# Weight products of one decoder layer: three products of 256 columns instead of one of 512 and one of 256

## Chip, core and metric

The kernel runs on one core of a Trainium2 chip. The metric is the device time of one execution in microseconds. Beside it stands the profile of one execution, taken by the hardware profiler, with the times of all instructions. PE is TensorE (matmuls), PEld its weight loads, DVE is VectorE, ACT is ScalarE, POOL is GpSimd.

## What is computed

One layer of a decoder on 256 tokens with 4096 channels, float32. The input is RMS-normalised and multiplied by `w_in` (4096 x 21024); the columns of the product are split into the inputs of two token mixers, of their gates and of the merge:

```
proj = einsum('btd,dn->btn', rms_norm(x, pre_norm_g), w_in)
o_a  = sliding_window_attention(q_a, k_a, v_a, sinks)         # 32 heads of 64
y_a  = einsum(o_a * silu(z_a), w_pa)                          # 2048 -> 4096
o_b  = rms_norm(gated_delta_rule(q_b, k_b, v_b, beta, g))     # 16 heads of 128
y_b  = einsum(o_b * silu(z_b), w_pb)                          # 2048 -> 4096
merged = sigmoid(gate_a) * y_a + sigmoid(gate_b) * y_b
out  = x + rms_norm(einsum(merged, w_o), post_norm_g)         # 4096 -> 4096
```

The q, k and v of branch B pass a causal convolution over four tokens and a SiLU first. Time goes almost wholly into the products with the four weight matrices, 492 MB read from HBM.

## The kernel before

**Precision by halves.** TensorE multiplies in the type `F32R`, which keeps fewer bits than float32. So every operand is split into a high part, rounded to `F32R`, and a low part, the rest. A product of weight w and activation h is then hi(w)hi(h) + hi(w)lo(h) + lo(w)hi(h). The activations of 256 tokens lie as one tile of 512 columns for each k tile: columns 0 to 255 the high part (`m[:, 0:T]`), columns 256 to 511 the low part (`m[:, T:512]`). Their names are `hT` for the input, `gbs` and `gas` for the gated outputs of the branches.

**The weight product.** `gemm` (L199) computes 512 output columns, 4 column tiles of 128, for all 256 tokens. The 128 x 128 tile of the weights is the stationary operand, the activations move. The contraction runs over 32 k tiles for `w_in` and 16 for `w_pa` and `w_pb`. `load` fetches four k tiles in one DMA of 1 MB, on SP's queue; `split` (L162 on) makes the two parts of two k tiles at a time: ACT casts the high part (L170), DVE subtracts for the low part (L171). Two k tiles times four column tiles are a unit, after which `tick` lets the side work advance by a stage. For each weight tile there are two matmuls, called a pair here:

- high part of the weights, all 512 columns of the activations, into all 512 columns of a PSUM bank (L227): columns 0 to 255 gather hi x hi, columns 256 to 511 gather hi x lo;
- low part of the weights, the 256 high columns, into columns 256 to 511 of the same bank (L228).

In the last k tile the two change places (L224, L225). One product occupies four banks, one for each column tile; the pool `psmain` has five, `psside` three for the side work.

**Folding.** The two halves of a bank have to be added. `fold` (L233) copies the right half to SBUF on ACT (L236), and either adds it to the left half on DVE (L238), or copies the left half too (L240) and adds the two in SBUF (L241). `scale_tokens` (L245) then multiplies four column tiles at once by `R`, the reciprocal root of each token's mean square, which is computed beside the first product (R is written at L319). The callers are the convolutions (`conv_silu`), the gates (`gate_silu`, `gate`), the inputs of the attention (`kv_chain`, `qa_chain`), and the merge of the branches (L703 to L708 and `merge`).

**Order of the work.** The Python order of the calls with priorities sets the order on each engine. `urgent(2)` puts the splitting of weights ahead of everything else, `urgent(1)` the folding ahead of the side work. The side work (chains such as `keys_chain`, `values_chain`, `heads_chain`) runs in stages between the units. The products come in this order: 16 of branch B's inputs with its mixer beside them (the substitution of the delta rule, L501 and L502, is DVE work beside the units 6 to 14 of a product), 8 of `gate_b`, 8 of `w_pb`, one for k and v of branch A and 8 for its gates and queries with the attention beside them, then `gate_a` in turn with `w_pa`. That makes 41 column blocks of `w_in` and 16 of the two branch projections. The output projection `w_o` has code of its own (L856 to L858): there the activations are stationary and 512 columns of the weights move.

Of the kernel before, what the change touches and what calls it, by code (L numbers as in the profile page):

```python
# [25 lines left out]
NEG = -1e30  # L26
WARM = (5, 2)  # products that warm the tensor engine up before and behind the first of x
PACED = 4  # the first pieces of x (and blocks of weights) that are queued in a fixed order
STEP = 1.5  # vector work of the substitution let in beside a unit of the weight product
STEP_UNITS = (6, 14)  # units of a product beside which the substitution runs  # L30
HELD = 8  # k tiles of the last output columns kept back, so that the first token tile ends early

# [21 lines left out]
def tile_hybrid_mixer(  # L54
# [20 lines left out]
    wp = ctx.enter_context(tc.tile_pool(name="weights", bufs=3, side="left"))  # L75
    ev = ctx.enter_context(tc.tile_pool(name="evac", bufs=4, side="left"))
    mp = ctx.enter_context(tc.tile_pool(name="psmain", bufs=5, space=PSUM))
    sp = ctx.enter_context(tc.tile_pool(name="psside", bufs=3, space=PSUM))
    dp = ctx.enter_context(tc.tile_pool(name="scratch", bufs=1, space=bass.MemoryType.DRAM))
# [7 lines left out]

# [1 line left out]
    ident = cp.tile([P, P], F32, name="ident")  # L89
# [37 lines left out]

# [1 line left out]
    chains = []  # L129
# [30 lines left out]

# [1 line left out]
    def split(raw, extra=False):  # L162
# [36 lines left out]
    def gemm(w, col0, mov, nkt, first=False):  # L199
        ps = [mp.tile([P, 512], F32, name="mm") for _ in range(4)]  # L200
        for k4 in range(nkt // 4):
            raw = load(w, k4, slice(col0, col0 + 512), (4, 2)[k4] if first and k4 < 2 else 1)
            if first:
                x_load(k4 + 1)
            if first and k4 == 0:
                parts = [split_first(raw[:, 2 * u:2 * u + 2], 2 * u) for u in range(2)]
            for u in range(2):
                if first and k4 == 0:
                    hi, lo = parts[u]
                elif first and k4 < PACED:  # L210
                    i = 4 * k4 + 2 * u - 3
                    with tc.issue_after(x_ins[i][0]), tc.issue_after(x_ins[i][1]):
                        hi, lo = split(raw[:, 2 * u:2 * u + 2])
                else:
                    hi, lo = split(raw[:, 2 * u:2 * u + 2])
                order = [(nt, kk) for nt in range(4) for kk in range(2)]
                if first and k4 == 0:
                    order = [(nt, kk) for kk in range(2) for nt in range(4)]
                for nt, kk in order:
                    c = slice(nt * P, nt * P + P)  # L220
                    kt = 4 * k4 + 2 * u + kk
                    m = mov(kt)
                    if kt == nkt - 1:
                        PE.matmul(ps[nt][:, T:512], lo[:, kk, c], m[:, 0:T], start=False, stop=False, skip_group_check=True)  # L224
                        PE.matmul(ps[nt], hi[:, kk, c], m, start=False, stop=True, skip_group_check=True)  # L225
                    else:
                        PE.matmul(ps[nt], hi[:, kk, c], m, start=(kt == 0), stop=False, skip_group_check=True)  # L227
                        newest["product"] = PE.matmul(ps[nt][:, T:512], lo[:, kk, c], m[:, 0:T], start=False, stop=False, skip_group_check=True).ins  # L228
                unit[0] = 2 * k4 + u
                tick()  # L230
        return ps

    def fold(dst, ps):  # L233
        with urgent(1):
            cr = ev.tile([P, T], F32, name="cr")
            S.copy(cr, ps[:, T:512])  # L236
            if dst is None:
                V.tensor_tensor(cr, ps[:, 0:T], cr, op=ALU.add)  # L238
            else:
                S.copy(dst, ps[:, 0:T])  # L240
                V.tensor_tensor(dst, dst, cr, op=ALU.add)  # L241
        return cr

    def scale_tokens(ap):
        V.tensor_tensor(ap, ap, mid(R, ap.shape[1]), op=ALU.mult)  # L245

# [9 lines left out]

# [1 line left out]
    gbf = gb.rearrange("p a b -> p (a b)")  # L258
# [64 lines left out]
    def start_chain():  # L323
# [53 lines left out]
        S.activation(beta, ab[:, :, 0:16], AF.Sigmoid)  # L377
        # softplus(z) = max(z, 0) + 2 atanh(e / (2 + e)), e = exp(-|z|)
        z = ws.tile([P, 2, H_B], F32, name="z")
# [21 lines left out]
        yield 11  # L401
        # exp of the running sums (second chunk) and of the sums behind (first chunk)
        pt = sp.tile([P, 512], F32, name="sd")
# [5 lines left out]

# [1 line left out]
    cin = ws.tile([P, 4, 260], F32, name="cin")  # L411
# [4 lines left out]
    def conv_silu(ps, tbase, dst):  # L416
        for nt in range(4):
            fold(cin[:, nt, 4:260], ps[nt])
        scale_tokens(cin[:, :, 4:260])
        for nt in range(4):  # L420
# [11 lines left out]
    def gate_silu(ps, dst, pool):  # L432
        for nt in range(4):
            fold(dst[:, nt], ps[nt])
        scale_tokens(dst)
        sg = pool.tile([P, 4, T], F32, name="sg")
        S.activation(sg, dst, AF.Sigmoid)
        V.tensor_tensor(dst, dst, sg, op=ALU.mult)

    def keys_chain(st, ps):  # L440
# [4 lines left out]
        yield 4 if h0 else 8  # L445
        # decays exp(sum of g over (s, c]), zero for c < s
        dec = ws.tile([P, 2, 4, P], F32, name="dec")
# [33 lines left out]
        G.tensor_tensor(nk.rearrange("p a b -> p (a b)"), k2.rearrange("p a b -> p (a b)"), phalf, op=ALU.pow)  # L481
        # inverse of I + B: 32 x 32 diagonal blocks by substitution, one system in a partition
        d1 = dp.tile([4, 8, 32, 32], F32, name="d1", bufs=2)
# [35 lines left out]
        yield 3  # L519
        # the rest by the nilpotent series over blocks  # L520
        X = ws.tile([P, 2, 4, P], F32, name="blx")
# [80 lines left out]
    def queries_chain(st, ps):  # L602
# [26 lines left out]
        for ch in range(2):  # L629
# [15 lines left out]
            yield 1  # L645
        # rms norm of o = o' / sqrt(128 (q2 + eps)), the factor taken under the root
        V.tensor_scalar(q2, q2, P * EPS, P * EPS * EPS, op0=ALU.mult, op1=ALU.add)
# [34 lines left out]

# [1 line left out]
    def gate(ps, dst):  # L684
        for nt in range(4):
            fold(dst[:, nt], ps[nt])
        scale_tokens(dst)
        S.activation(dst, dst, AF.Sigmoid)
# [14 lines left out]
    for c in range(8):  # L703
        ps = gemm(w_pb, 512 * c, lambda kt: gbs[:, kt], KTB)
        for nt in range(4):
            y = fold(None, ps[nt])
            with urgent(1):
                V.tensor_tensor(m[c][:, nt], m[c][:, nt], y, op=ALU.mult)  # L708
    gspool.__exit__(None, None, None)
    gbpool.__exit__(None, None, None)  # L710

# [1 line left out]
    gapool = tc.tile_pool(name="gapool", bufs=1, side="right")  # L713
# [8 lines left out]
    def kv_chain(ps):  # L722
        for nt in range(4):
            fold(kv[:, nt], ps[nt])
        scale_tokens(kv)
        nc.sync.dma_start(kx[0:64], kv[64:128, 0:2])
        nc.sync.dma_start(kx[64:128], kv[0:64, 0:2])
        yield 3
        pt = side((2, T))
        for c in range(2):  # L730
            for t in range(2):
                PE.transpose(pt[:, c, t * P:t * P + P], kv[:, 2 + t, c * P:c * P + P], ident)
        S.copy(vt, pt)
# [7 lines left out]
    def qa_chain(st, ps):  # L741
        q = ap.tile([P, 4, T], F32, name="q")
        for nt in range(4):
            fold(q[:, nt], ps[nt])
        scale_tokens(q)
        yield 2
# [5 lines left out]
    def heads_chain(st, nt):  # L752
        g, q, gz = st["g"], st["q"], st["gz"]
        hs = slice(8 * g + 2 * nt, 8 * g + 2 * nt + 2)
        s = ap.tile([P, 2, 384], F32, name="s", bufs=2)
        # the two heads of a pair hold different rows of the array and alternate
        pts = [sp.tile([P, 512], F32, name="sd") for _ in range(2)]
# [48 lines left out]

# [1 line left out]
    ps = gemm(w_in, OFF_GA, movh, KT)  # L808
# [11 lines left out]
    def merge(c):  # L820
        ps = gemm(w_pa, 512 * c, lambda kt: gas[:, kt], KTB)
        for nt in range(4):
            y = fold(None, ps[nt])
            with urgent(1):
                V.tensor_tensor(y, y, sa[c][:, nt], op=ALU.mult)
                V.tensor_tensor(m[c][:, nt], m[c][:, nt], y, op=ALU.add)

# [15 lines left out]

# [1 line left out]
    op_ = ctx.enter_context(tc.tile_pool(name="outp", bufs=1, side="left"))  # L845
# [105 lines left out]
```

## Time and profile before

| what | value |
|---|---|
| time, median of 3 runs | 2700.98 us (2700.91 to 2701.2) |
| span of the profiled execution, first to last instruction | 2699.4 us |
| PE busy | 2685.1 us, 15294 matmuls |
| PEld busy | 2331.5 us, 15294 weight loads |
| DVE busy | 1640.3 us |
| ACT busy | 1277.8 us |
| mean granted TensorE clock | 0.999 |
| mean HBM traffic | 184 GB/s |

The profiled execution's own time is its span, 1.6 us below the median of the runs. A row of a group of instructions gives line, engine, operation, output<-inputs, shapes and count, then busy time and the mean duration of one in ns, then the engine's idle time just before them and what ended it. The records of successive matmuls overlap (a mean of 393 ns for one of 512 columns, with the next one starting some 230 ns behind it); how fast they follow each other is read from their start times. A few per cent of the matmul records are missing.

### The profile page before, as it was taken

To read this page: it belongs to the slowest core of one execution; us is meant where nothing else is said; L and a number is where in the kernel's file an instruction comes from. 1 tells how busy PE (TensorE), PEld (TensorE's weight loads), DVE (VectorE), ACT (ScalarE), POOL (GpSimd) and SP (SyncE) were. 2 spreads that over 40 slices of the span, in tenths; PEclk is the share of its full clock that TensorE was granted. 3 is DMA by queue.
4 is the path that set the end of the run, shared out by engine and by line. 5 is a ranking of instruction groups with operands and counts; after the bars stand their busy time and mean duration, and the time that the engine had idled before them with its cause. 6 is when DMAs were issued, how large, how long until landed. Compare 5 with 4: busy or idle time off the path is not lost.

```text
span 2699.4 us, 37887 instructions
## 1 busy us (share of the span) xinstructions
PE 2685.1 (99%) x15294; PEld 2331.5 (86%) x15294; DVE 1640.3 (61%) x2273; ACT 1277.8 (47%) x1866; POOL 38.5 (1%) x58
## 2 busy tenths in 40 slices
PE   9999999999999999999999999999999999999998
PEld 8888888888888888888888888888888888888886
DVE  7785876776776454555555665666555555644445
ACT  6445545545545444444444554555444445443433
POOL 0100100000000000000000000000000000000000
PEclk9999999999999999999999999999999999999999
DMA  8554554655555655566565455455555555765555
GB/s 269 168 180 157 181 176 157 195 162 171 182 175 165 194 188 187 188 190 191 193 194 188 156 178 167 156 186 169 191 187 187 189 192 186 248 230 188 187 187 172
DMA packets 261856, 499.90 MB, mean 185 GB/s; under 512 B 21936, under 2 KB 23088, under 8 KB 261040
## 3 DMA queue, kind: packets, MB, share of 16 engines
q1 hardware_dynamic: 260528, 495.37, 57.3%
q8 instruction: 120, 1.97, 0.3%
q10 hardware_dynamic: 1152, 2.10, 0.2%
q14 instruction: 56, 0.46, 0.0%
HBM read 491.93 MB, written 5.24 MB: 184 GB/s over the span
## 4 chain that ended last, share of the span: by engine, by line
PE 93%; DVE 6%; issue 1%; ACT 0%; DMA 0%; POOL 0%; SPq 0%; DVEq 0%; POOLq 0%; ACTq 0%
PE mm L227 47%; PE mm L228 25%; PE mm L857 4%; PE mm L858 4%; PE mm L856 4%; DVE lo L171 2%; PE mm L225 2%; DVE pr L501 1%; PE mm L224 1%; DVE xs L502 1%; PE sd L762 1%; PE sd L797 1%; PE sd L546 0%; PE sd L787 0%; DVE c L427 0%
## 5 line engine op out<-in xcount | busy, mean ns | idle before, releaser
L227 PE MATMUL mm<-hT,hi 128*128 128x512 f32 x5084 | 1790.2, 393 | 0.1
L171 DVE TENSOR_TENSOR lo<-raw,hi 128x1024 fp32r<-128x1024 f32 x909 | 1111.3, 1224 | 901.5 <-ACT hi L170 900.3
L170 ACT CAST hi<-raw 128x1024 fp32r<-128x1024 f32 x909 | 952.6, 1049 | 1281.0 <-PE mm L227 1049.6
L228 PE MATMUL mm<-hT,lo 128*128 128x256 f32 x5084 | 1436.1, 283 | 1.2 <-DVE lo L171 0.6
L227 PEld LDWEIGHTS mm<-hT,hi 128*128 128x128 f32 x5084 | 954.4, 188 | 198.9 <-issue 7.9
L228 PEld LDWEIGHTS mm<-hT,lo 128*128 128x128 f32 x5084 | 960.5, 189 | 14.9 <-DVE lo L171 7.0
L858 PE MATMUL mm<-hi,ms 128*128 128x512 f32 x508 | 200.9, 396 | 0.0
L857 PE MATMUL mm<-lo,ms 128*128 128x512 f32 x508 | 200.9, 396 | 0.0
L856 PE MATMUL mm<-hi,ms 128*128 128x512 f32 x508 | 200.9, 395 | 0.0
L227 PE MATMUL mm<-gas,hi 128*128 128x512 f32 x480 | 168.0, 390 | 0.0
L227 PE MATMUL mm<-gbs,hi 128*128 128x512 f32 x480 | 168.0, 390 | 0.0
L228 PE MATMUL mm<-gbs,lo 128*128 128x256 f32 x480 | 135.3, 282 | 0.0
L228 PE MATMUL mm<-gas,lo 128*128 128x256 f32 x480 | 135.3, 282 | 0.0
L857 PEld LDWEIGHTS mm<-lo,ms 128*128 128x128 f32 x508 | 95.4, 188 | 23.3
L858 PEld LDWEIGHTS mm<-hi,ms 128*128 128x128 f32 x508 | 95.4, 188 | 23.0
L856 PEld LDWEIGHTS mm<-hi,ms 128*128 128x128 f32 x508 | 95.4, 188 | 23.0
L227 PEld LDWEIGHTS mm<-gas,hi 128*128 128x128 f32 x480 | 90.1, 188 | 17.8
L227 PEld LDWEIGHTS mm<-gbs,hi 128*128 128x128 f32 x480 | 90.1, 188 | 17.8
L236 ACT COPY cr<-mm 128x256 f32<-128x256 f32 x228 | 83.8, 368 | 18.5 <-PE mm L225 16.4
L228 PEld LDWEIGHTS mm<-gbs,lo 128*128 128x128 f32 x480 | 90.7, 189 | 1.3
L228 PEld LDWEIGHTS mm<-gas,lo 128*128 128x128 f32 x480 | 90.7, 189 | 1.4
L225 PE MATMUL mm<-hT,hi 128*128 128x512 f32 x164 | 64.2, 392 | 0.0
(265 smaller groups left out, 1434.9 us busy)
## 6 DMA issues: line engine op xcount, KB each, us to landing
raw<-in_w_in_dram SPq DMA_DIRECT2D x326, 1024.0 KB, 5.1
raw<-in_w_o_dram SPq DMA_DIRECT2D x64, 1024.0 KB, 5.5
raw<-in_w_pb_dram SPq DMA_DIRECT2D x32, 1024.0 KB, 5.5
raw<-in_w_pa_dram SPq DMA_DIRECT2D x32, 1024.0 KB, 5.5
xr<-in_x_dram SPq DMA_DIRECT2D x4, 1024.0 KB, 7.7
xt<-in_x_dram SPq DMA_DIRECT2D x7, 512.0 KB, 11.2
blx<-d SPq DMA_DIRECT2D x16, 128.0 KB, 5.6
pg<-in_post_norm_g_dram SPq DMA_DIRECT2D x1, 2048.0 KB, 7.1
```

Source lines behind the costliest of these rows:

```text
L170: newest["hi"] = S.copy(hi, raw).ins
L171: newest["lo"] = V.tensor_tensor(lo, raw, hi.bitcast(F32), op=ALU.subtract).ins
L224: PE.matmul(ps[nt][:, T:512], lo[:, kk, c], m[:, 0:T], start=False, stop=False, skip_group_check=True)
L225: PE.matmul(ps[nt], hi[:, kk, c], m, start=False, stop=True, skip_group_check=True)
L227: PE.matmul(ps[nt], hi[:, kk, c], m, start=(kt == 0), stop=False, skip_group_check=True)
L228: newest["product"] = PE.matmul(ps[nt][:, T:512], lo[:, kk, c], m[:, 0:T], start=False, stop=False, skip_group_check=True).ins
L236: S.copy(cr, ps[:, T:512])
L501: V.tensor_tensor(pr[:, :, 0:i + 1], xs3[:, :, 0:i + 1], mid(bl3[:, i, 0:i + 1], 8), op=ALU.mult)
L502: V.tensor_reduce(xs3[:, :, i], pr[:, :, 0:i + 1], axis=AX.X, op=ALU.add, negate=True)
L856: PE.matmul(ps[t], mt[:, ts], hi, start=(kt == 0), stop=False)
L857: PE.matmul(ps[t], mt[:, ts], lo, start=False, stop=False)
L858: PE.matmul(ps[t], mt[:, tl], hi, start=False, stop=(kt == KT - 1))
```

## The change

Each weight tile gets three matmuls of 256 columns that add into the same 256 PSUM columns: hi x hi, hi x lo, lo x hi. Two column tiles share a bank, so a product needs two banks; `psmain` has four banks instead of five, `psside` four instead of three. Nothing is left to be folded: `scaled` multiplies a whole bank (two column tiles) by `R` on DVE, straight from PSUM, and the merges read PSUM in the same way. The last k tile has the order of all others. `urgent(1)` now covers the multiplication by `R` too. Comments are also removed.

```diff
-    ev = ctx.enter_context(tc.tile_pool(name="evac", bufs=4, side="left"))
-    mp = ctx.enter_context(tc.tile_pool(name="psmain", bufs=5, space=PSUM))
-    sp = ctx.enter_context(tc.tile_pool(name="psside", bufs=3, space=PSUM))
+    ev = ctx.enter_context(tc.tile_pool(name="evac", bufs=2, side="left"))
+    mp = ctx.enter_context(tc.tile_pool(name="psmain", bufs=4, space=PSUM))
+    sp = ctx.enter_context(tc.tile_pool(name="psside", bufs=4, space=PSUM))
...
     def gemm(w, col0, mov, nkt, first=False):
-        ps = [mp.tile([P, 512], F32, name="mm") for _ in range(4)]
+        ps = [mp.tile([P, 512], F32, name="mm") for _ in range(2)]
...
                     m = mov(kt)
-                    if kt == nkt - 1:
-                        PE.matmul(ps[nt][:, T:512], lo[:, kk, c], m[:, 0:T], start=False, stop=False, skip_group_check=True)
-                        PE.matmul(ps[nt], hi[:, kk, c], m, start=False, stop=True, skip_group_check=True)
-                    else:
-                        PE.matmul(ps[nt], hi[:, kk, c], m, start=(kt == 0), stop=False, skip_group_check=True)
-                        newest["product"] = PE.matmul(ps[nt][:, T:512], lo[:, kk, c], m[:, 0:T], start=False, stop=False, skip_group_check=True).ins
+                    dst = ps[nt // 2][:, nt % 2 * T:nt % 2 * T + T]
+                    PE.matmul(dst, hi[:, kk, c], m[:, 0:T], start=(kt == 0 and nt % 2 == 0), stop=False, skip_group_check=True)
+                    PE.matmul(dst, hi[:, kk, c], m[:, T:512], start=False, stop=False, skip_group_check=True)
+                    newest["product"] = PE.matmul(dst, lo[:, kk, c], m[:, 0:T], start=False, stop=(kt == nkt - 1), skip_group_check=True).ins
...
-    def fold(dst, ps):
+    def pair(bank):
+        return bank.rearrange("p (a b) -> p a b", a=2)
+
+    def scaled(dst, ps):
         with urgent(1):
-            cr = ev.tile([P, T], F32, name="cr")
-            S.copy(cr, ps[:, T:512])
-            if dst is None:
-                V.tensor_tensor(cr, ps[:, 0:T], cr, op=ALU.add)
-            else:
-                S.copy(dst, ps[:, 0:T])
-                V.tensor_tensor(dst, dst, cr, op=ALU.add)
-        return cr
-
-    def scale_tokens(ap):
-        V.tensor_tensor(ap, ap, mid(R, ap.shape[1]), op=ALU.mult)
+            for j in range(2):
+                V.tensor_tensor(dst[:, 2 * j:2 * j + 2], pair(ps[j]), mid(R, 2), op=ALU.mult)
...
     def gate(ps, dst):
-        for nt in range(4):
-            fold(dst[:, nt], ps[nt])
-        scale_tokens(dst)
+        scaled(dst, ps)
         S.activation(dst, dst, AF.Sigmoid)
...
         ps = gemm(w_pb, 512 * c, lambda kt: gbs[:, kt], KTB)
-        for nt in range(4):
-            y = fold(None, ps[nt])
+        for j in range(2):
+            mj = m[c][:, 2 * j:2 * j + 2]
             with urgent(1):
-                V.tensor_tensor(m[c][:, nt], m[c][:, nt], y, op=ALU.mult)
+                V.tensor_tensor(mj, mj, pair(ps[j]), op=ALU.mult)
...
         ps = gemm(w_pa, 512 * c, lambda kt: gas[:, kt], KTB)
-        for nt in range(4):
-            y = fold(None, ps[nt])
+        for j in range(2):
+            mj = m[c][:, 2 * j:2 * j + 2]
             with urgent(1):
-                V.tensor_tensor(y, y, sa[c][:, nt], op=ALU.mult)
-                V.tensor_tensor(m[c][:, nt], m[c][:, nt], y, op=ALU.add)
+                y = ev.tile([P, 2, T], F32, name="y")
+                V.tensor_tensor(y, pair(ps[j]), sa[c][:, 2 * j:2 * j + 2], op=ALU.mult)
+                V.tensor_tensor(mj, mj, y, op=ALU.add)
```

The other callers of `fold` and `scale_tokens` call `scaled` in the same way as `gate`.

More of the change, by code (lines that the diff above doesn't have):

```diff
@@ L416, in conv_silu @@
     def conv_silu(ps, tbase, dst):
-        for nt in range(4):
-            fold(cin[:, nt, 4:260], ps[nt])
-        scale_tokens(cin[:, :, 4:260])
+        scaled(cin[:, :, 4:260], ps)
         for nt in range(4):
@@ L684, in gate @@
     def gate(ps, dst):
-        for nt in range(4):
-            fold(dst[:, nt], ps[nt])
-        scale_tokens(dst)
+        scaled(dst, ps)
         S.activation(dst, dst, AF.Sigmoid)
@@ L704, in tile_hybrid_mixer @@
         ps = gemm(w_pb, 512 * c, lambda kt: gbs[:, kt], KTB)
-        for nt in range(4):
-            y = fold(None, ps[nt])
+        for j in range(2):
+            mj = m[c][:, 2 * j:2 * j + 2]
             with urgent(1):
-                V.tensor_tensor(m[c][:, nt], m[c][:, nt], y, op=ALU.mult)
+                V.tensor_tensor(mj, mj, pair(ps[j]), op=ALU.mult)
     gspool.__exit__(None, None, None)
@@ L722, in kv_chain @@
     def kv_chain(ps):
-        for nt in range(4):
-            fold(kv[:, nt], ps[nt])
-        scale_tokens(kv)
+        scaled(kv, ps)
         nc.sync.dma_start(kx[0:64], kv[64:128, 0:2])
@@ L742, in qa_chain @@
         q = ap.tile([P, 4, T], F32, name="q")
-        for nt in range(4):
-            fold(q[:, nt], ps[nt])
-        scale_tokens(q)
+        scaled(q, ps)
         yield 2
@@ L821, in merge @@
         ps = gemm(w_pa, 512 * c, lambda kt: gas[:, kt], KTB)
-        for nt in range(4):
-            y = fold(None, ps[nt])
+        for j in range(2):
+            mj = m[c][:, 2 * j:2 * j + 2]
             with urgent(1):
-                V.tensor_tensor(y, y, sa[c][:, nt], op=ALU.mult)
-                V.tensor_tensor(m[c][:, nt], m[c][:, nt], y, op=ALU.add)
+                y = ev.tile([P, 2, T], F32, name="y")
+                V.tensor_tensor(y, pair(ps[j]), sa[c][:, 2 * j:2 * j + 2], op=ALU.mult)
+                V.tensor_tensor(mj, mj, y, op=ALU.add)
     for c in range(1, 8):
```

## Prediction

> **What bounds the kernel now.** I read the page first: busy times, granted clock, the chain that ended last.
>
> ```profile
> span 2699.4 us, 37887 instructions
> PE 2685.1 (99%) x15294; PEld 2331.5 (86%) x15294; DVE 1640.3 (61%) x2273; ACT 1277.8 (47%) x1866; POOL 38.5 (1%) x58
> PEclk9999999999999999999999999999999999999999
> PE 93%; DVE 6%; issue 1%; ACT 0%; DMA 0%; POOL 0%; SPq 0%; DVEq 0%; POOLq 0%; ACTq 0%
> PE mm L227 47%; PE mm L228 25%; PE mm L857 4%; PE mm L858 4%; PE mm L856 4%; DVE lo L171 2%; PE mm L225 2%; DVE pr L501 1%; PE mm L224 1%; DVE xs L502 1%; PE sd L762 1%; PE sd L797 1%; PE sd L546 0%; PE sd L787 0%; DVE c L427 0%
> ```
>
> TensorE is busy from end to end, and the lines that the change rewrites (L224 to L228) hold three quarters of the chain. A busy matmul record may still hide waiting, because a record is longer than the distance to the next one. So I looked at a stretch without side work by windows (columns: stretch, then busy time and count of PE, PEld, DVE, ACT, POOL, then clock, DMA share and GB/s), and then at the start times of the matmuls in it.
>
> ```profile
> 1100.00:1200.00 100.00, 100.00 (x579) 88.51 (x578) 51.86 (x54) 45.87 (x59) 0.00 (x0) 1.00 0.60 190
> ```
>
> The next rows are the timeline of PE alone over the last unit of one product and the start of the next (start us, duration us, line, output<-moving, stationary). The moving operand has 512 columns for the high part of a weight tile (L227, L225) and 256 for the low part (L228, L224).
>
> ```profile
> 1171.97 0.39 PE L227 MATMUL mm<-hT,hi 128*128 128x512 f32 x1
> 1172.20 0.28 PE L228 MATMUL mm<-hT,lo 128*128 128x256 f32 x1
> 1172.32 0.28 PE L224 MATMUL mm<-hT,lo 128*128 128x256 f32 x1
> 1172.44 0.39 PE L225 MATMUL mm<-hT,hi 128*128 128x512 f32 x1
> 1172.67 0.39 PE L227 MATMUL mm<-hT,hi 128*128 128x512 f32 x1
> 1172.90 0.28 PE L228 MATMUL mm<-hT,lo 128*128 128x256 f32 x1
> 1173.01 0.28 PE L224 MATMUL mm<-hT,lo 128*128 128x256 f32 x1
> 1173.13 0.39 PE L225 MATMUL mm<-hT,hi 128*128 128x512 f32 x1
> 1173.36 0.39 PE L227 MATMUL mm<-hT,hi 128*128 128x512 f32 x1
> 1173.59 0.28 PE L228 MATMUL mm<-hT,lo 128*128 128x256 f32 x1
> 1173.71 0.28 PE L224 MATMUL mm<-hT,lo 128*128 128x256 f32 x1
> 1173.83 0.39 PE L225 MATMUL mm<-hT,hi 128*128 128x512 f32 x1
> 1174.05 0.39 PE L227 MATMUL mm<-gbs,hi 128*128 128x512 f32 x1
> ```
>
> From 1171.97 to 1174.05 lie six pairs (one 512, one 256): 2.08 us, 346.7 ns a pair. The step behind a 256 is 0.12, 0.12, 0.11, 0.12, 0.12, 0.12 us: 0.71 over six, 118.3 ns. A 512 therefore takes 346.7 - 118.3 = 228.4 ns. There is no waiting in these rows: the pace is TensorE's own, at a granted clock of 1.00. The kernel is bound by the number and the length of its matmuls.
>
> **The change, part by part.**
>
> *The products.* Each pair becomes three products of 256 columns, and each matmul has its own weight load:
>
> ```profile
> L227 PEld LDWEIGHTS mm<-hT,hi 128*128 128x128 f32 x5084 | 954.4, 188 | 198.9 <-issue 7.9
> L228 PEld LDWEIGHTS mm<-hT,lo 128*128 128x128 f32 x5084 | 960.5, 189 | 14.9 <-DVE lo L171 7.0
> ```
>
> The columns streamed stay 768; what is added is one matmul and one load per pair. How often: w_in is 41 column blocks of 512 x 32 k tiles x 4 column tiles = 5248 pairs, w_pa and w_pb 16 x 16 x 4 = 1024; together 6272 (the trace has a few per cent fewer records).
>
> The price hangs on the step of a 256 that follows a 256. The last-unit rows show exactly this form: L228 then L224, two products of 256 with different loads into the same 256 PSUM columns, 0.12, 0.11 and 0.12 us apart, and a third load behind them, 0.12 us later each time. So neither accumulating into columns just written nor two loads in a row slows anything there. Three at 118.3 are 355.0 ns, 8.3 ns more than 346.7. Times 6272: +52 us.
>
> Bounds: linear in columns, the added 256 columns of a 512 cost 228.4 - 118.3 = 110.1 ns, and 8.2 ns are a fixed cost. Were that fixed cost to vanish in a run of 256s, three would take 330.3 ns: -103 us. At the other end stands the output product, 512 behind 512:
>
> ```profile
> 2399.70 0.40 PE L858 MATMUL mm<-hi,ms 128*128 128x512 f32 x1
> 2399.94 0.40 PE L856 MATMUL mm<-hi,ms 128*128 128x512 f32 x1
> ...
> 2401.80 0.40 PE L858 MATMUL mm<-hi,ms 128*128 128x512 f32 x1
> ```
>
> Nine steps in 2.10 us, 233.3 ns; less 110.1 that is 123.2 for a 256, and three are 369.6: +22.9 ns, +144 us. I take 118.3, because it is read from the very form that will run; a ns up or down in it is 3 x 6272 ns = 19 us.
>
> Why an extra matmul isn't free can be seen where a load came late (PE and PEld in one timeline):
>
> ```profile
> 556.36 0.19 PEld L228 LDWEIGHTS mm<-hT,lo 128*128 128x128 f32 x1 [0.31 <-DVE lo L171]
> 556.36 0.39 PE L228 MATMUL mm<-hT,lo 128*128 128x256 f32 x1
> 556.47 0.19 PEld L224 LDWEIGHTS mm<-hT,lo 128*128 128x128 f32 x1
> 556.59 0.28 PE L224 MATMUL mm<-hT,lo 128*128 128x256 f32 x1
> ```
>
> The next load may start 0.11 us behind the late one, and its matmul starts 0.12 us later. A load that nothing hides costs about 0.11 us, as much as the 110.1 ns that 256 columns stream. Under a 512 the load has slack; under a 256 it has next to none, and the change leaves only 256s.
>
> The Trainium skill says this too, in "TensorE: Matmul & The Clock Gate", section "LDWEIGHTS (loading the stationary operand)": the load takes its columns over 1.2 GHz, 107 ns for 128; the 0.11 us above agrees. Its section "Back-to-back issue gap" speaks for a cheaper change: N / 2.4 + 2.5 ns, so only 2.5 ns for one more matmul, and by it the sum would be about +16 us; by the rows it is +52, and the 118.3 and 228.4 ns measured lie above its 109 and 216.
>
> *The folding.* It goes: 4 folds in each of 57 products, with two copies on ACT in most and an add on DVE, and the scaling by R. In come two DVE operations per product that read a whole bank.
>
> ```profile
> L236 ACT COPY cr<-mm 128x256 f32<-128x256 f32 x228 | 83.8, 368 | 18.5 <-PE mm L225 16.4
> L238 DVE TENSOR_TENSOR cr<-mm,cr 128x256 f32<-128x256 f32 x64 | 25.4, 417 | 0.0
> L245 DVE TENSOR_TENSOR m<-m,R 128x1024 f32<-128x1024 f32 x8 | 9.8, 1226 | 0.3
> L866 DVE TENSOR_TENSOR u<-mm,pg 128x512 f32<-128x512 f32 x16 | 11.0, 688 | 3.6 <-ACT jk L862 3.6
> ```
>
> In a product with R, DVE had 4 x 0.42 + 1.23 = 2.9 us and gets 2 x 0.69 = 1.4; ACT loses up to 8 x 0.37 = 3.0 us. All of this lies beside TensorE (DVE 52 and ACT 46 of 100 us in the stretch above), so it is worth nothing there. It counts only where DVE paces the weight tiles, in the substitution of branch B (chain of waits: start, duration):
>
> ```profile
> 552.03 1.23 DVE lo L171
> 555.08 1.23 DVE lo L171
> 558.24 1.22 DVE lo L171
> 561.48 1.23 DVE lo L171
> ```
>
> Here a unit takes 3.15 us, against 8 x 346.7 ns = 2.77. The longer unit of 8 x 355 ns = 2.84 hides under 3.15: 0.07 us saved in each of some twenty such units, 1.4 us. What TensorE lost to late tiles is in the waits:
>
> ```profile
> PEld mm L228 <- DVE lo L171: 7.0, 17, 0.5
> PEld mm L227 <- ACT gz L240: 1.0, 3, 0.3
> ```
>
> So the relief is worth 0 to 8 us; with the hiding I take 2 us off. Without the cover of TensorE the two bank reads would cost 1.4 us per product, 57 x 1.4 = 80 us, but that needs a wait for a bank.
>
> *Banks.* A product takes two of four banks instead of four of five, so the next one starts in the other two and evacuation has a whole product (22 or 44 us) instead of 0.69 us. No row of TensorE's waits names an evacuation, so nothing is gained; one side bank more gains nothing either. The first evacuation now needs R; R is there before the first fold (so no DVE wait ahead of later weight tiles; if it came late, they would wait for it once, a few us):
>
> ```profile
> 56.20 0.42 DVE L319 COPY R<-sd 128x256 f32<-128x256 f32 x1
> 57.76 0.85 DVE L241 TENSOR_TENSOR cin<-cin,cr 128x256 f32<-128x256 f32 x2
> ```
>
> The swapped order of the last k tile goes too; its rows keep the 346.7 ns, so 0. No DMA is added or moved, and the output product stays as it is.
>
> **Sum.** 2699.4 + 52 - 2 = 2749.4 us of span. The runs' median, 2701.0, lies 1.6 us above the span, so 2751.
>
> **Rivals.**
> 1. *No slower: the repeated load is cheap.* The first two products of a triple have the same stationary tile. If the second needed no load of its own, it would cost the 110.1 ns of its columns: 118.3 + 110.1 + 118.3 = 346.7, no change; with 8 us of late tiles recovered about 2693. It decides as soon as the mean step falls under 115.6 ns. For it: the load is what has no slack. Against: L856 and L857 have the same stationary slice of ms one after the other, and each step in the output rows is 0.23 us, as to L858, which has another.
> 2. *A smaller fixed cost.* The 8.2 ns are a difference of steps read to 10 ns. If a run of 256s pays only a third of it, 2.7 ns for the added matmul, the change costs 6272 x 2.7 ns = 17 us: 2718. For it: a 512 takes nearly twice a 256. Against: the six steps would have to average 116.5 instead of 118.3 ns, and their sum of 0.71 us would be 0.70. The gap that the Trainium skill gives, named above, comes to about this.
> 3. *Three loads in a row pile up.* The rows show runs of only two 256s. If each settles toward 123.2, the time is 2701 + 144 = 2845; at 120, 2701 + 83 = 2784. For it: in 100 us PEld is busy 88.5 and will be nearer full. Against: the third step is 0.12 like the first.
>
> **How the numbers follow.** Forecast 75% (step 117.3 to 119.6: 2730 to 2778), rival 1 9%, rival 2 5%, rival 3 11%, half of it under 2790. The range 2714 to 2790 takes in rival 2 and the nearer half of rival 3 and leaves out about 14%. A difference under 0.2% (5.4 us) isn't told from none: same 5% and faster 4% (rival 1 without and with the recovered tiles, and 1% for what I did not think of), slower 91%.
>
> **What would show it.** Steps of 118 ns throughout, 355 ns a triple, a product of w_in in 45.5 us instead of 44.4 where no side work runs, and of w_pb in 22.7 instead of 22.2. As many loads as matmuls, about 6272 more of each. ACT about 146 us less busy (228 x 0.37 + 164 x 0.38), TensorE still near 99% busy. I am wrong if the step is under 116 ns or over 120, if loads are fewer than matmuls, or if TensorE waits for a bank or for DVE more than before.

## The result, and the profile after

The changed kernel takes 2727.96 us (median of four runs, 2727.4 to 2728.2) against 2701.09 us: a ratio of 1.0098, interval 1.0086 to 1.0110. It is slower by 27 us; 50 were forecast. Two executions at a lower granted clock count in no comparison: one of the kernel with the products apart (2916.5 us at 0.85) and one of the kernel before (4005.7 us at 0.62). The page of after, its head and its chain:

```profile
span 2726.2 us, 49677 instructions
PE 2709.2 (99%) x21566; PEld 2615.2 (96%) x21566; DVE 1564.9 (57%) x2038; ACT 1160.5 (43%) x1474; POOL 37.8 (1%) x58
PE 95%; DVE 3%; issue 1%; DMA 0%; ACT 0%; SPq 0%; DVEq 0%; POOLq 0%; POOL 0%
PE mm L225 26%; PE mm L227 26%; PE mm L226 26%; PE mm L841 4%; PE mm L842 4%; PE mm L843 4%; DVE lo L171 1%; DVE pr L491 1%; DVE xs L492 1%; PE sd L746 1%; PE sd L781 0%; PE sd L536 0%; PE sd L771 0%; PE sd L283 0%; PE sd L358 0%
```

6272 matmuls and as many loads have come in (21566 against 15294). No row of these products is missing in the trace of before: the 5084 rows of L227 and the 164 of L225, which is the last k tile, are the 5248 that the prediction counts for `w_in`. TensorE is as full as before, and its share of the chain has risen from 93 to 95%. So the answer lies in the step from one product to the next. The timeline of PE in the gate_b stage, where nothing else runs on TensorE:

```profile
1040.03 0.28 PE L225 MATMUL mm<-hT,hi 128*128 128x256 f32 x1
1040.15 0.28 PE L226 MATMUL mm<-hT,hi 128*128 128x256 f32 x1
1040.27 0.28 PE L227 MATMUL mm<-hT,lo 128*128 128x256 f32 x1
1040.38 0.28 PE L225 MATMUL mm<-hT,hi 128*128 128x256 f32 x1
...
1041.08 0.28 PE L225 MATMUL mm<-hT,hi 128*128 128x256 f32 x1
```

Three triples take 1.05 us, 350 ns each. Over a longer stretch the count in a window tells the step more exactly: the window counts every record that overlaps it, and a record is 0.28 us long, so the step is 100.28 us over the count. Two windows of after, in the gate_b stage and in the last stage (gate_a with w_pa); the columns are those of the prediction's window row:

```profile
1000.00:1100.00 100.00, 100.00 (x859) 100.00 (x858) 47.95 (x42) 40.12 (x39) 0.00 (x0) 1.00 0.57 187
2000.00:2100.00 100.00, 100.00 (x851) 100.00 (x851) 46.80 (x42) 38.09 (x37) 0.00 (x0) 1.00 0.57 186
```

859 matmuls are a step of 116.7 ns, a triple of 350.0; 851 are 117.8 and 353.5. By the start times of the matmuls gate_b (from its second product) and w_pb run at 350.0 ns and the last stage at 353.3. The last stage is the 7 products of gate_a from the second on and the 8 of w_pa, 1408 triples. Branch B and the attention lie between. The 5991 triples that nothing interrupts average 351.5 ns. Against 346.7 that is 4.8 ns, times 6272 some 30 us. The span grew by 26.8, so about 3 us came back elsewhere.

Where the time went can be read from the distance between the first matmul of one stage and that of the next (us; the first product of gate_a, which the attention's work accompanies, is counted with the attention). The last two columns are kernels that the experiments explain:

| stage | weight tiles | before | after | cut alone | one start |
|---|---|---|---|---|---|
| ahead of the first product | - | 6.8 | 7.0 | 7.0 | 8.0 |
| branch B | 2048 | 805.9 | 815.2 | 818.9 | 815.1 |
| gate_b and w_pb | 1536 | 539.1 | 544.1 | 544.0 | 544.1 |
| attention | 1280 | 488.2 | 491.5 | 493.6 | 491.5 |
| last stage | 1408 | 490.0 | 499.1 | 494.4 | 494.4 |
| output product and end | - | 369.4 | 369.4 | 369.4 | 369.4 |

From before to after a weight tile costs 3.3 ns more in gate_b and w_pb, 6.4 in the last stage, 4.5 in branch B and 2.6 in the attention.

In the waits of the weight loads the one for ACT's copy of gz (1.0 us) is gone:

```profile
PEld mm L225 <- issue: 8.0, 32, 0.3
PEld mm L227 <- DVE lo L171: 6.5, 13, 0.8
```

TensorE's own waits for late low parts have grown all the same; the first row is before, the second after:

```profile
PE mm L228 <- DVE lo L171: 0.6, 3, 0.2
```

```profile
PE mm L227 <- DVE lo L171: 3.6, 8, 0.6
```

Open after this: whether the products alone are the cost, what sets a step of 116.7 ns, why the last stage is slower, and what the folding was worth.

### The profile page after: what moved, and what is told of

Its sections match the earlier page's. It is cut to its first block, busy times and chain, and to the rows that moved or that the text cites. A ratio compares the mean times of both kernels' runs of the same rounds, so it can differ in the third digit from the quotient of the medians.

```text
span 2726.2 us, 49677 instructions
## 1 busy us (share of the span) xinstructions
PE 2709.2 (99%) x21566; PEld 2615.2 (96%) x21566; DVE 1564.9 (57%) x2038; ACT 1160.5 (43%) x1474; POOL 37.8 (1%) x58
## 4 chain that ended last, share of the span: by engine, by line
PE 95%; DVE 3%; issue 1%; DMA 0%; ACT 0%; SPq 0%; DVEq 0%; POOLq 0%; POOL 0%
PE mm L225 26%; PE mm L227 26%; PE mm L226 26%; PE mm L841 4%; PE mm L842 4%; PE mm L843 4%; DVE lo L171 1%; DVE pr L491 1%; DVE xs L492 1%; PE sd L746 1%; PE sd L781 0%; PE sd L536 0%; PE sd L771 0%; PE sd L283 0%; PE sd L358 0%
## 5 line engine op out<-in xcount | busy, mean ns | idle before, releaser
L225 PE MATMUL mm<-hT,hi 128*128 128x256 f32 x5248 | 1480.0, 282 | 0.0
L227 PE MATMUL mm<-hT,lo 128*128 128x256 f32 x5248 | 1469.1, 280 | 3.9 <-DVE lo L171 3.6
L226 PE MATMUL mm<-hT,hi 128*128 128x256 f32 x5248 | 1466.0, 279 | 0.0
L225 PEld LDWEIGHTS mm<-hT,hi 128*128 128x128 f32 x5248 | 987.7, 188 | 9.0 <-issue 8.0
L227 PEld LDWEIGHTS mm<-hT,lo 128*128 128x128 f32 x5248 | 987.0, 188 | 6.8 <-DVE lo L171 6.5
L226 PEld LDWEIGHTS mm<-hT,hi 128*128 128x128 f32 x5248 | 988.2, 188 | 0.4
L227 PE MATMUL mm<-gas,lo 128*128 128x256 f32 x512 | 144.0, 281 | 0.0
L225 PE MATMUL mm<-gas,hi 128*128 128x256 f32 x512 | 143.5, 280 | 0.0
L227 PE MATMUL mm<-gbs,lo 128*128 128x256 f32 x512 | 143.0, 279 | 0.0
L226 PE MATMUL mm<-gbs,hi 128*128 128x256 f32 x512 | 143.0, 279 | 0.0
L225 PE MATMUL mm<-gbs,hi 128*128 128x256 f32 x512 | 143.0, 279 | 0.0
L226 PE MATMUL mm<-gas,hi 128*128 128x256 f32 x512 | 142.4, 278 | 0.0
L225 PEld LDWEIGHTS mm<-gas,hi 128*128 128x128 f32 x512 | 96.4, 188 | 0.0
L226 PEld LDWEIGHTS mm<-gas,hi 128*128 128x128 f32 x512 | 96.4, 188 | 0.0
```

The costliest lines, as they stand in the source:

```text
L225: PE.matmul(dst, hi[:, kk, c], m[:, 0:T], start=(kt == 0 and nt % 2 == 0), stop=False, skip_group_check=True)
L226: PE.matmul(dst, hi[:, kk, c], m[:, T:512], start=False, stop=False, skip_group_check=True)
L227: newest["product"] = PE.matmul(dst, lo[:, kk, c], m[:, 0:T], start=False, stop=(kt == nkt - 1), skip_group_check=True).ins
```

## Experiments

**The cut alone.** The kernel before, with the product of 512 cut into two of 256 and all else kept:

```diff
-PE.matmul(ps[nt], hi[:, kk, c], m, start=(kt == 0), ...)
+PE.matmul(ps[nt][:, 0:T], hi[:, kk, c], m[:, 0:T], start=(kt == 0), ...)
+PE.matmul(ps[nt][:, T:512], hi[:, kk, c], m[:, T:512], ...)
```

> The kernel before with one edit: the product of 512 columns is cut into two of 256, into the two halves of the same bank; banks, folding and order stay. Theory A (the cost lies in the products alone, one more matmul with its load per weight tile, 3.3 to 6.7 ns a triple as the trace of after shows): 2701 + 21 to 42 us, 2722 to 2743, within 8 us of after, and steps of 116.7 to 117.8 ns. Theory B (a triple costs the 355 ns forecast, and the removed folding gave about 25 us back): 2750, steps of 118.3 ns.

Measured: 2730.07 us, ratio 1.0107 (1.0090 to 1.0124). The cost lies in the products, as theory A has it. Its windows (here in the same two stages) have the step of 350.0 ns a triple in both:

```profile
1000.00:1100.00 100.00, 100.00 (x860) 100.00 (x859) 48.33 (x46) 45.14 (x57) 0.00 (x0) 1.00 0.60 190
2000.00:2100.00 100.00, 100.00 (x859) 100.00 (x858) 53.57 (x63) 42.40 (x50) 0.00 (x0) 1.00 0.60 190
```

Its undisturbed triples average 350.7 ns: 25 us by the products. Its span grew by 28.0, so it lost 3 us elsewhere, where after won 3. The table of stages says the same: after is 3.7 us shorter than this kernel in branch B and 2.0 in the attention, and 4.6 longer in the last stage, at its slower pace. The folding with its four-of-five banks therefore costs some 6 us more, beside a TensorE that runs 256s, than what the change put in its place.

**The folding alone.** The kernel before, products kept, evacuation by one DVE operation on the left half:

```diff
-            cr = ev.tile([P, T], F32, name="cr")
-            S.copy(cr, ps[:, T:512])
-            ...
+            V.tensor_tensor(dst, ps[:, 0:T], R, op=ALU.mult)
```

> The kernel before with its products of 512 and 256 columns, but no folding: the evacuation reads only the left half of each bank (the sums of the low parts are left out), multiplied by R on DVE straight from PSUM, with no copies on ACT. Theory A: the folding was hidden, the relief is worth 0 to 8 us: 2693 to 2701. Theory B (the relief gave back half of the forecast cost): about 2676.

Measured: 2704.87 us, ratio 1.0014 (1.0004 to 1.0023). Neither: it is 3 us slower. 164 + 228 copies fewer bring no gain: TensorE now waits for banks, as the waits of its weight loads show (the second row):

```profile
PEld mm L228 <- DVE lo L171: 5.8, 10, 0.8
PEld mm L227 <- DVE cin L237: 5.8, 8, 1.8
```

**One copy less.** The kernel before, the left half added by DVE straight from PSUM:

```diff
-                S.copy(dst, ps[:, 0:T])
-                V.tensor_tensor(dst, dst, cr, op=ALU.add)
+                V.tensor_tensor(dst, ps[:, 0:T], cr, op=ALU.add)
```

> The kernel before, its products kept, with one copy less per fold: the left half is no longer copied by ACT, DVE adds it straight from PSUM (164 ACT copies of 0.378 us go, 62 us of ACT). If the evacuation is worth something it shows here without the third product: 2697 to 2701; if it is hidden, as its place beside a TensorE that is 99% busy says, 2701, no difference. A version faster than both kernels would have to come from here.

Measured: 2719.8 us, ratio 1.0068 (1.0055 to 1.0080): 18 us slower by taking 164 copies away. Its waits:

```profile
PEld mm L227 <- DVE cin L240: 12.1, 4, 3.1
```

Four times, once in each group of branch B, the next product needs a bank that still waits for its turn on DVE, about 3 us each: 12 of the 18 us. Behind three of these four pauses the granted clock is 0.50 for a while:

```profile
369.60:373.00 3.40, 3.40 (x13) 2.81 (x12) 3.02 (x5) 0.45 (x1) 0.00 (x0) 0.50 0.96 308
571.00:577.80 6.80, 5.83 (x18) 4.96 (x19) 5.31 (x9) 1.80 (x4) 0.00 (x0) 0.50 0.54 174
775.80:779.20 3.40, 3.17 (x10) 2.68 (x11) 3.37 (x7) 0.00 (x0) 0.00 (x0) 0.50 0.69 210
```

In the first of these stretches a pair takes 0.64 us by its start times, where it takes 0.35 at the clock of 1.00. At that pace 13.6 us hold some 6 us less work, about the rest of the 18. Behind the first of the four pauses, at 163 us, the clock stays at 1.00. ACT's second copy looked like waste and was what emptied the banks in time. In the changed kernel no wait names an evacuation, with DVE alone emptying the banks. Its next product starts in two others; that this is the reason is likely, but no run changed the banks alone.

**Order.** The changed kernel with the products of one stationary tile apart:

```diff
 PE.matmul(dst, hi[:, kk, c], m[:, 0:T], ...)
+PE.matmul(dst, lo[:, kk, c], m[:, 0:T], ...)
 PE.matmul(dst, hi[:, kk, c], m[:, T:512], ...)
-PE.matmul(dst, lo[:, kk, c], m[:, 0:T], ...)
```

> The changed kernel with the order high x high, low x high, high x low, so that the two products with the same stationary tile are no longer neighbours. Theory A (every matmul pays for its own load, whatever stood before it): the same as after, within the 21 us that lie between triples of 350.0 and of 353.3 ns: 2722 to 2743, most likely 2728. Rival (a repeated load is cheaper, which is why the step came out under 118.3 ns): triples of 355 ns, about 2750.

Measured: 2725.14 us (three executions, 2725.07 to 2726.15), ratio 1.0089 (1.0072 to 1.0106). The steps are read from another execution of the same kernel:

> The same kernel as the one with the order high x high, low x high, high x low, for a profile at the full granted clock, which the first look lacked. Theory A: clean triples of 350.0 or 353.3 ns, a mean of 349.5 to 352, no difference between the step behind a repeated stationary tile and the others that the order moves with it; about 2726.

Measured: 2724.48 us (2723.27 and 2725.69), 350.0 ns a triple in gate_b, w_pb and the last stage, a mean of 350.6. A repeated stationary tile is no cheaper: apart, the products cost no more than as neighbours. The some 3 us less than after come from the last stage: at 350.0 instead of 353.3 ns it is 4.7 us shorter, and 2.4 us are lost ahead of and in branch B.

**Load or stream.** Three changed kernels tell the two limits apart. First, twice the loads for the same columns: each product cut into two of 128 columns.

```diff
-PE.matmul(dst, hi[:, kk, c], m[:, 0:T], ...)
+PE.matmul(dst[:, 0:128], hi[:, kk, c], m[:, 0:128], ...)
+PE.matmul(dst[:, 128:256], hi[:, kk, c], m[:, 128:256], ...)
```

> The changed kernel with each product of 256 columns cut again into two of 128: the same columns streamed, twice the loads. Theory A (a load of 128 columns takes as long as 256 columns stream, and binds below that): each step stays at 108 to 117 ns, a weight tile takes 650 to 700 ns, the time is 2728 + 6272 x (300 to 350 ns) = 4600 to 4920 us. Rival (streaming binds and a matmul adds a fixed 8 to 10 ns): six steps of 62 to 64 ns, 378 ns, about 2900 us.

Measured: 4748.26 us (one run). A window of it (100.28 us over 898, a step of 111.7 ns):

```profile
2000.00:2100.00 100.00, 100.00 (x898) 100.00 (x897) 23.43 (x20) 20.38 (x20) 0.00 (x0) 1.00 0.30 96
```

Half the columns, and nearly the same step. Next, half the load for the same columns:

```diff
+w0 = P if kt == 0 else 64
+r = slice(0, w0)
+c0 = slice(nt * P, nt * P + w0)
-PE.matmul(dst, hi[:, kk, c], m[:, 0:T], ...)
+PE.matmul(dst[r], hi[:, kk, c0], m[:, 0:T], ...)
```

> The changed kernel with stationary tiles of 64 columns instead of 128 in all k tiles but the first (half of the output columns then sum one k tile only): the same moving columns, half the load. Theory A (in a run of 256s the load of 128 columns is what sets the step): the step falls from 117 ns to 107 to 111, a triple from 351 to 321 to 333, and the time by 31/32 (or 15/16) x 6272 x 18 to 30 ns = 110 to 185 us, to 2543 to 2618. Rival (a fixed cost of handing over from one product to the next, whatever the load): steps stay at 117 ns, 2728.

Measured: 2738.3 us, ratio 1.0136 (1.0118 to 1.0154). Theory A falls: the step does not get shorter, by stages it is 117 to 119 ns on the mean. Two windows of it, in gate_b (851, 117.8 ns) and in the last stage (860, 116.6 ns):

```profile
1000.00:1100.00 100.00, 100.00 (x851) 100.00 (x850) 45.46 (x39) 39.70 (x38) 0.00 (x0) 1.00 0.58 185
2000.00:2100.00 100.00, 100.00 (x860) 100.00 (x859) 49.50 (x46) 38.69 (x37) 0.00 (x0) 1.00 0.59 187
```

So the load does not set the step of a 256. That left open what the 111.7 ns of the six products were, a load or a least time of any matmul. Last, both halved:

```diff
+PE.matmul(dst[r, 0:128], hi[:, kk, c0], m[:, 0:128], ...)
+PE.matmul(dst[r, 128:256], hi[:, kk, c0], m[:, 128:256], ...)
```

> The changed kernel with six products of 128 columns for each weight tile and stationary tiles of 64 columns in all k tiles but the first (half of the output columns then sum one k tile only). In the run with six products of 128 and full loads a step took 112.5 ns, in the one with half loads and 256 columns 118. Theory C (two limits lie side by side: a load of 128 columns takes 112 ns, 256 columns take 107 to 110 ns and some 8 to 12 ns to hand over, and in after the second one binds): with both halved a step takes 62 to 70 ns, a weight tile 370 to 420, the time 2738 + 6272 x (20 to 70 ns) = 2860 to 3180 us. Rival (every product takes some 112 ns at least, whatever its load): steps of 112 ns, 4740 us.

Measured: 2941.76 us (one run). A window of it:

```profile
1000.00:1100.00 100.00, 100.00 (x1611) 100.00 (x1610) 43.01 (x37) 37.50 (x36) 0.00 (x0) 1.00 0.57 180
```

Its records are 0.22 us long; 100.22 us over 1611 are 62.2 ns (by stages it is 62 to 64): there is no least time of 112, so the 111.7 ns were the load of 128 columns. Two limits lie side by side. A load of 128 columns needs 111.7 ns, 256 moving columns need 116.7 ns. How a step divides into a price of its columns and a fixed cost of the matmul is not settled. From 128 to 256 columns it grows by 54.5 ns, which would leave 7.7 ns fixed. From 256 to 512, by the 233.3 ns of the output product (there activations are stationary and weights move), it grows by 116.7, which leaves nothing fixed.

**The slow last stage.** The changed kernel with 29 transposes of a constant: one ahead of each product from the second of gate_b to the last but one of w_pa, but for those of the attention:

```diff
+    def between():
+        PE.transpose(side()[:, 0], ident, ident)
...
+        between()
         gate(gemm(w_in, OFF_GA + 512 * c, movh, KT), sa[c])
+        between()
         merge(c - 1)
```

> The changed kernel with one transpose of the constant ident put ahead of each product from the second of gate_b to the last of w_pa but those of the attention (29 transposes, whose results nobody reads). In after all triples of the stages gate_b and w_pb take 350.0 ns on the mean and all of gate_a and w_pa 353.3. Theory A (the pace is a state into which TensorE falls at a start and which it keeps until something else runs on it): with 29 new starts products of both stages show both paces; the time is 2728 + 29 x 0.3 us - 0 to 5 us = 2731 to 2737. Rival (the pace belongs to the stage, through the places of its operands): 350.0 and 353.3 ns stay where they are, 2737.

Measured: 2728.09 us (one run), no gain in time. But the pace of the last stage changed; the first row is this kernel, the second the one with a single transpose, which follows:

```profile
2000.00:2100.00 100.00, 100.00 (x860) 100.00 (x859) 47.49 (x43) 38.74 (x37) 0.00 (x0) 1.00 0.58 186
```

```profile
2000.00:2100.00 100.00, 100.00 (x860) 100.00 (x859) 47.06 (x42) 38.70 (x37) 0.00 (x0) 1.00 0.60 190
```

Both stages now run at 350.0 ns (but for one product, the first of w_pa, at 353.3). The mixture that theory A expected did not come: new starts led nearly always to the faster pace. The rival falls too: the operands lie where they did, and the last stage is no longer slow. So one start should do:

```diff
     for c in range(1, 8):
+        if c == 1:
+            PE.transpose(side()[:, 0], ident, ident)
         gate(gemm(w_in, OFF_GA + 512 * c, movh, KT), sa[c])
```

> The changed kernel with a single transpose of the constant ident (its result unread) ahead of the second product of the last stage, gate_a and w_pa, whose triples all take 353.3 ns in after and 350.0 with a transpose ahead of each product. Theory A (a state that TensorE keeps until something else runs on it; one new start is enough to change it): the 14 or 15 products behind it run at 350.0 ns, 1408 triples x 3.3 ns = 4.7 us less, and 0.3 us more: 2723.5. Rival (each product needs a new start, or the stage falls back): 353.3 ns but for the first product, 2728.

Measured: 2723.64 us (2722.95 to 2725.88), ratio to the kernel before 1.0082 (1.0068 to 1.0096), the 4.3 us less than after that were expected. One matmul that does nothing takes the pace of 15 products from 353.3 to 350.0 ns. Up to the transpose the two kernels are the same, and the five executions of this one and the four of after do not overlap. With the kernel that keeps the products apart it is the fastest of the versions with three products, and still 22 us slower than the kernel before; none of the runs beat that.

## Why the prediction was right, and where it was wrong

- **The time.** 2728 us lies in the range of 2714 to 2790, but between the forecast's own band of 2730 to 2778 and rival 2. That it came so near the band is in part luck: 4.6 us of it are the slower pace of the last stage, which nobody foresaw.
- **The bound.** Right: TensorE's own pace sets the time before and after, and the cut alone reproduces the loss.
- **The products.** The sign and the mechanism were right, the term was mis-sized: +52 us forecast, 30 measured (25 without the slower pace). The step that failed is "three at 118.3 are 355.0 ns". The 118.3 ns was taken from runs of two 256s "because it is read from the very form that will run". It was not that form: those two always stand behind a 512. In a run of nothing but 256s the step is 116.7 ns, in its slower pace 117.8. The prediction's rows did hold a run of one length, the 512s of the output product at 233.3 ns, and half of that is 116.7. It took 110.1 ns off it for the added 256 columns, but that figure belongs to the alternating rows. By the two uniform runs a 512 and a 256 would be 233.3 + 116.7 = 350.0 ns, what three 256s take; the alternating pair of before takes 346.7. By these figures it is the pair that is 3.3 ns cheaper than its parts, and the change gives that up. Why it is cheaper was not tested, and the 233.3 ns come from other operands.
- **Why an extra matmul isn't free.** Wrong: the forecast blamed the load that "under a 256" has next to no slack. The late load of 0.11 us was read correctly, and 111.7 ns with six products confirms it as a limit. But it lies just under the 116.7 ns of the stream and does not bind; halving it gains nothing.
- **The two rules of the Trainium skill.** In "TensorE: Matmul & The Clock Gate", the section "LDWEIGHTS (loading the stationary operand)" gives 107 ns for 128 columns, near the 111.7 measured. The section "Back-to-back issue gap" gives 2.5 ns for one more matmul, in a formula for the gap of an isolated one, and that came nearer the 3.3 ns of the faster pace than the 8.3 forecast, though both of its gaps (109 and 216 ns) lie below the steps measured, 116.7 and 228.4.
- **The folding.** The sum had -2 us, from bounds of 0 to 8. Against the cut alone, which keeps the folding, the change is worth some 6 us, so the bounds hold. But the gain did not come where the prediction put it, in the substitution, where the longer unit was to hide under 3.15 us. There the unit of after takes 3.4 us (chain of waits: start, duration):

```profile
553.05 1.22 DVE lo L171
556.42 1.21 DVE lo L171
560.09 1.22 DVE lo L171
563.28 1.23 DVE lo L171
```

So nothing was saved there: TensorE's own waits for low parts are 3.6 us, up from 0.6. Why the unit grew was not tested. "Nothing is gained" by the banks was too little: with four of five banks and DVE emptying them the kernel before lost 3 us (no copy on ACT) and 18 us (one copy on ACT).

- **Rival 1** (repeated load cheap): refuted, the order makes no difference, and the mean step did not fall under 115.6 ns. **Rival 2** (a smaller fixed cost, 2.7 ns): nearest to the truth, 3.3 ns, with 9 us more for the stretches at the slower pace (30 less 6272 x 3.3 ns = 21). Its counter-argument rested on six steps of the wrong form. **Rival 3** (loads pile up): no; the third product is no slower than the first.
- **The signs named beforehand.** As many loads as matmuls, 6272 more: yes. A triple of 355 ns: no, 350.0 to 353.3. ACT less busy by 146 us: 117 by the page, where the records of successive copies overlap and such time counts once; the durations of all ACT instructions fell by 147 in sum. TensorE waiting for DVE more than before was named as a sign of being wrong, and it does, by the 3 us above. It does not wait for a bank.

## What to carry to other kernels

A duration taken from a mixed sequence is not the duration in a uniform one: here 1.6 ns in 118 more than halved the term (21 us at the faster pace instead of 52). When a count of thousands multiplies a small difference, look in the trace for a run of one length and take the step from it: here half the step of a 512 behind a 512 would have given 350.0 ns and +21 us. That is one case, seen afterwards. And before an evacuation is called hidden, look at how soon its bank is needed: a copy that seems superfluous may be the one that empties it.

## What was not expected of the hardware

A run of products has two paces, 350.0 and 353.3 ns a triple, with the same instructions and operands; the second lasted over 1408 triples, and with a single transpose ahead of them it did not come. What decides which pace a start leads to was not found: in branch B and the attention, where side work interrupts all the time, both occur.

A load of 128 columns (111.7 ns) and the stream of 256 (116.7 ns) are nearly equal, so products of 128 columns with full stationary tiles gain next to nothing: half the columns saved 5 ns of 117.

In the kernel with one copy less, pauses of TensorE of 3 us were followed by 3.4 or 6.8 us at a granted clock of 0.50, three times in four.
